# A hybrid attention and mLSTM layer: first stage in written order, pieces of the weights ahead of x, gate row before the gate chain, decays in halves, loads tied behind matmuls

## The chip, the cores and the metric

The kernel runs on one core of a Trainium2 chip. A core has five engines that work side by side: TensorE (PE) for matmuls, VectorE (DVE), ScalarE (ACT), GpSimd (POOL) and SyncE (SP), which here only issues DMAs. Each engine works off its own instructions in the order in which they were emitted, so an instruction that waits holds everything behind it on the same engine; that holds for a DMA issue on SP, ACT or POOL too. The metric is the device time of one execution in microseconds (us), the median of several runs; less is better.

## The reference

One layer for a sequence of 2048 tokens of width 1024, in float32:

```
c_act = silu(c)
shift, scale, gate = split(c_act @ w_ada + b_ada, 3)
h = rmsnorm(x, norm_w) * (1 + scale) + shift
proj = h @ w_in + b_in
na_q, na_k, na_v, na_z, ml_q, ml_k, ml_v, ml_o, ml_z, i_f, f_f, i_b, f_b = split(proj)
na_out = neighbourhood_attention(na_q, na_k, na_v, rpb) * silu(na_z)      # 32 x 64 grid, 8 heads
mq, mk = split(silu(short_conv(concat(ml_q, ml_k), conv_w, conv_b)))
hm = mlstm(mq, mk, ml_v, i_f, f_f) + flip(mlstm(flip(mq), flip(mk), flip(ml_v), flip(i_b), flip(f_b)))
ml_out = layernorm(hm * sigmoid(ml_o)) * ml_norm_w * silu(ml_z)           # 4 heads of 128
out = rmsnorm(x + gate * (concat(na_out, ml_out) @ w_out), final_norm_w)
```

## The kernel before

Every large product is made of three matmuls in a reduced float32 type: each operand is split into a high part (a rounded copy) and a low part (the rest), and high x high, high x low and low x high are added up in PSUM. So h is kept as hhi and hlo in four groups of 512 tokens, and a weight block as whi and wlo in one of two slots (a and b). A block of w_in is 256 columns; `load_w` (line 188) brings it in two halves, each a DMA, a high copy on ACT and a subtraction on POOL.

**First stage** (`start`, line 198). Shift and scale come from w_ada in 32 pieces of 128 x 512 (`ada_tile`, line 232): DVE multiplies each by a column of silu(c) and adds it to `acc`; at the end of a quarter `columns` (line 242) sums `acc` over the partitions with four matmuls against ones, and ACT, POOL or DVE add the bias and, for the scale, 1 and norm_w, into shT and gT. There are four quarters: (part, q) with part 1 the scale, part 0 the shift, and q the half of the 1024 features. x comes in sixteen tiles of 128 tokens; `prep_x` (line 217) squares them on ACT, takes the reciprocal root by Newton steps (`rsqrt`, line 1181; on POOL for the first four tiles, on DVE else) and scales x. PE transposes the scaled x feature by feature, and h = gT * x + shT is written as hhi (ACT) and hlo (POOL or DVE). For group 0 the first four features' tiles are done (`first_h`, line 264) and multiplied into four PSUM tiles (`vo_first`, line 473) before the other half of shift and scale is there (`scaled`, `shifted`). For later groups `make_h` (line 282) runs as a side chain: while `vo_group` (line 485) makes the products of block 1 with group g, each of its four token tiles advances the chain by a step that makes two features of h of group g + 1. `vo_group` evacuates each PSUM tile on DVE (line 499) into a staging tile of two, which is stored to DRAM when it is next flushed.

**Token blocks** (`tok_blocks`, line 557): blocks 2 to 5, four groups of four token tiles each; each token tile advances `self.chain` by one step (64 in all). The chain was the gate chain (decay logarithms, scans, line 577) and then `decays` (line 685): 16 groups of 128 x 1024 with two tiles, each loaded by two broadcast DMAs on SP, masked on POOL, raised by eight ACT exponentials and stored by two DMAs on ACT's queue. Between its steps ran `gate_row` (line 391), the third part of shift, scale and gate: eight 128 x 1024 pieces of w_ada in two buffers, summed on DVE. In the same time SP issues the small copies that build the bias tables (lines 528 and 551).

**Convolution blocks** (`conv_blocks`, line 752): blocks 6 to 9, eight tiles of 24 matmuls over 512 tokens each, a five tap convolution on DVE, SiLU on ACT, and for k a transpose on PE (line 819).

**mLSTM stage** (`phase1b`, line 929): per head two passes over chunks of 128 tokens, with the remaining projections (`nq_gen`, line 845) pumped between them as filling for PE. `close_step` (line 990) runs once per chunk and finishes older chunks; it also takes a job at every other step: eight loads of finished keys (`kk_jobs`, line 974). The gate values z come back in one tile (`load_z`, line 1063), are multiplied into the result, and the tile is stored to d_mix on ACT's queue (line 1155).

**Attention and output** (`phase2`, line 1206) follow in an order written by hand.

What sets the order: outside `manual_schedule` a planner places the instructions of each engine, by its own costs and estimates of when inputs are ready; tile releases and DMA landings become waits. Inside `manual_schedule` each engine gets its instructions as they are written. Before, only the last stage (line 1591) was in written order. The first stage began so:

```python
        for tt in range(4):
            load_x(tt)
        prep_x([0, 1, 2, 3])
        for kt in range(KT):
            ada_tile(1, 0, kt)
            if kt == 2:
                nc.sync.dma_start(bada, self.b_ada)
                nc.sync.dma_start(nw, self.norm_w)
        self.load_w(0, 0, (0,))
```

## Time and profile before

| | us |
|---|---|
| median of 3 runs | 1383.26 (1382.79 to 1388.96) |
| the profiled execution | 1385.16 |
| its span, first to last instruction | 1383.4 |
| PE busy in it | 1291.3 |
| mean granted clock of PE | 0.989 of full speed |

In the rows below PE, DVE, ACT, POOL and SP are the engines, PEld is PE's loading of weights, and SPq or ACTq with a DMA name is the issue of a DMA on that engine. A row of a timeline gives the start, the duration, the engine, the line, the operation, out<-in with shapes, how many such instructions follow each other, and in brackets how long the engine had been idle and what released it. A row of waits gives who waited for whom, the sum, how often, and the longest. The granted clock is a share of TensorE's full clock.

### The profile page before, as it was taken

What the parts mean: (1) busy time and instruction counts of PE and PEld (TensorE: products, weight loads), DVE (VectorE), ACT (ScalarE), POOL (GpSimd) and SP (SyncE); (2) the same over time, 40 slices, a digit from 0 to 9 for tenths busy, and PEclk for the clock granted to TensorE, in tenths of its full rate; (3) what the DMA queues carried; (4) which work ended last, traced back from release to release, by engine and by line L of the source; (5) the groups of instructions that cost most, each with busy time, mean ns of one, the idle gap of its engine ahead of it and who ended that gap; (6) DMA issues with size and microseconds to landing.
All of it is one profiled execution on the core that took longest, in us unless ns stands there. A gap on an engine that the chain in (4) does not pass through costs nothing.

```text
span 1383.4 us, 23357 instructions
## 1 busy us (share of the span) xinstructions
PE 1291.3 (93%) x8204; PEld 1104.9 (80%) x8204; DVE 792.3 (57%) x2428; ACT 531.8 (38%) x1123; POOL 284.1 (21%) x306
## 2 busy tenths in 40 slices
PE   2989998998999999999989999899998999999996
PEld 2889998998887778788878878778876777778775
DVE  6683324111355569246767866767736666667664
ACT  4642334423232233213313322323346555555552
POOL 4343212424101011001212101212201211112121
PEclk9999999999999999999999999999999999999998
DMA  9799449787557685554675788555588996867871
GB/s 321 223 290 228 122 97 238 175 204 189 149 110 210 151 191 160 164 157 144 184 219 182 229 237 284 165 159 159 176 249 251 209 228 171 187 184 183 205 182 47
DMA packets 243272, 263.29 MB, mean 190 GB/s; under 512 B 31814, under 2 KB 200006, under 8 KB 243154
## 3 DMA queue, kind: packets, MB, share of 16 engines
q1 hardware_dynamic: 151774, 186.18, 49.8%
q0 software_dynamic: 20496, 36.21, 10.8%
q10 hardware_dynamic: 70884, 39.40, 9.9%
q8 instruction: 65, 1.06, 0.3%
q14 instruction: 53, 0.43, 0.1%
HBM read 177.18 MB, written 92.72 MB: 195 GB/s over the span
## 4 chain that ended last, share of the span: by engine, by line
PE 46%; DMA 11%; issue 4%; DVE 4%; POOL 1%; ACT 1%; ACTq 0%; SPq 0%; DVEq 0%; POOLq 0%
PE pq L866 19%; PE y L1429 9%; DMA tab<-d_t 4%; PE pT L1369 3%; PE pO L1384 2%; PE pS L1341 2%; PE pi L1090 2%; DMA kv<-d_ck 2%; PE px L1088 2%; PE pc L429 2%; PE pc L430 2%; PE pc L431 2%; DMA d_mix<-zt 2%; PE dc L1036 1%; DMA d_qna<-qst 1%
## 5 line engine op out<-in xcount | busy, mean ns | idle before, releaser
L866 PE MATMUL pq<-hhi,whi_a 128*128 128x512 f32 x512 | 208.6, 407 | 1.2 <-ACT u L773 0.8
L866 PE MATMUL pq<-hlo,whi_a 128*128 128x512 f32 x512 | 208.9, 408 | 0.0
L866 PE MATMUL pq<-hhi,wlo_a 128*128 128x512 f32 x512 | 208.2, 407 | 0.0
L866 PEld LDWEIGHTS pq<-hhi,whi_a 128*128 128x128 f32 x512 | 97.3, 190 | 18.9 <-ACT u L773 1.2
L866 PEld LDWEIGHTS pq<-hlo,whi_a 128*128 128x128 f32 x512 | 97.2, 190 | 16.8 <-issue 0.5
L866 PEld LDWEIGHTS pq<-hhi,wlo_a 128*128 128x128 f32 x512 | 97.3, 190 | 16.6
L1371 ACT ACTIVATE pt<-pT 96x384 f32<-96x384 f32 (+3 forms) x128 | 65.8, 514 | 84.5 <-PE pT L1369 81.3
L1350 ACT ACTIVATE pbuf<-pbuf,mn 128x480 f32<-128x480 f32 (+5 forms) x128 | 76.1, 595 | 54.1 <-DVE mn L1349 53.8
L1429 PE MATMUL y<-hhi,whi_a 128*128 128x512 f32 x256 | 90.6, 415 | 0.5 <-ACT whi_a L1399 0.5
L1429 PE MATMUL y<-hhi,wlo_a 128*128 128x512 f32 (+1 forms) x272 | 90.6, 399 | 0.2 <-ACT y L1436 0.2
L1349 DVE CUSTOM_DVE_ANT_0 pbuf<-pS,tab 128x480 f32<-128x480 f32 (+5 forms) x128 | 63.3, 540 | 40.3 <-PE pS L1341 29.6
L840 POOL TENSOR_TENSOR wlo_a<-rawq,whi_a 128x1024 fp32r<-128x1024 f32 x20 | 48.6, 2430 | 169.8 <-ACT whi_a L839 144.9
L1112 POOL TENSOR_TENSOR hm<-hm,ck 128x128 f32<-128x128 f32 x64 | 26.4, 413 | 260.3 <-DVE hm L1111 183.4
L429 PE MATMUL pvo<-whi_b,hhi 128*128 128x256 f32 x256 | 74.1, 289 | 5.7 <-DVE stvo L499 5.7
L1093 ACT ACTIVATE num<-px,gtile 128x129 f32<-128x129 f32 x120 | 38.3, 366 | 105.7 <-PE px L1088 88.0
L1020 DVE TENSOR_SCALAR wv<-kv,gtile 128x129 f32<-128x129 f32 x120 | 38.4, 329 | 67.1 <-DMA kv<-d_ck 33.5
L1369 PE MATMUL pT<-ident,pbuf 128*128 128x128 f32 (+2 forms) x416 | 66.8, 273 | 10.0 <-DVE pbuf L1361 8.5
L1369 PEld LDWEIGHTS pT<-ident,pbuf 128*128 128x128 f32 (+2 forms) x416 | 50.3, 136 | 31.9 <-issue 11.6
L430 PE MATMUL pvo<-wlo_b,hhi 128*128 128x256 f32 x256 | 72.8, 285 | 0.0
L431 PE MATMUL pvo<-whi_b,hlo 128*128 128x256 f32 x256 | 72.8, 284 | 0.0
L714 ACT ACTIVATE dec<-dec,gtile 128x128 f32<-128x128 f32 x128 | 42.0, 392 | 71.4 <-POOL dec L710 68.3
L499 DVE TENSOR_TENSOR stvo<-pvo,brow 128x256 f32<-128x256 f32 x64 | 26.5, 419 | 68.6 <-PE pvo L431 56.4
(295 smaller groups left out, 3432.6 us busy)
## 6 DMA issues: line engine op xcount, KB each, us to landing
ck<-d_ck SPq DMA_DIRECT2D x64, 384.5 KB
kv<-d_ck SPq DMA_DIRECT2D x120, 128.5 KB
rawq<-in_w_main_dram SPq DMA_DIRECT2D x28, 512.0 KB
raw<-in_w_main_dram SPq DMA_DIRECT2D x20, 512.0 KB
d_ck<-stvo SPq DMA_DIRECT2D x16, 514.0 KB
x<-in_x_dram SPq DMA_DIRECT2D x16, 512.0 KB
wada<-in_w_ada_dram SPq DMA_DIRECT2D x32, 256.0 KB
dec<-d_mneg SPq DMA_DIRECT2D x32, 256.0 KB
```

Of the source, the lines that this page charges most:

```text
L429: nc.tensor.matmul(ps, lhi(k), rhi(k), start=(k == 0), stop=False)
L430: nc.tensor.matmul(ps, lhi(k), rlo(k), start=False, stop=False)
L431: nc.tensor.matmul(ps, llo(k), rhi(k), start=False, stop=(k == KT - 1))
L714: nc.scalar.activation(t[:, d, o, :], t[:, d, o, :], AF.Exp, bias=self.cols["g"][:, d, h, c : c + 1])
L840: nc.gpsimd.tensor_tensor(lo[:, :, cs], raw, hi[:, :, cs].bitcast(F32), ALU.subtract)
L866: nc.tensor.matmul(patch_ps(ps) if patch else ps, w, self.htok(h, g, k, patch), start=(k == 0 and n == 0), stop=(k == KT - 1 and n == 2))
L1020: nc.vector.tensor_scalar(wv, tiles[d, i][:, 128:257], self.cols["w"][:, d, h, c : c + 1], None, ALU.mult)
L1349: nc.vector.tensor_tensor_reduce(pt[:, :nk], ps, tabs[place[u]][j][:, :nk], 1.0, 3e38, ALU.add, ALU.min, mn)
L1350: nc.scalar.activation(pt[:, :nk], pt[:, :nk], AF.Exp, bias=mn, scale=-1.0, accum_out=sums[:, j : j + 1])
L1369: nc.tensor.transpose(ps[:cs, i, :], U[u][j][:, i * cs : (i + 1) * cs], self.ident)
L1371: nc.scalar.activation(t[:cs, :nch, :], ps[:cs, :nch, :], AF.Copy)
L1429: nc.tensor.matmul(y, m[:, k, :], w[k][:, cs], start=(k == 4 and n == 0), stop=(k == 3 and n == 2))
```

## The change

The first stage runs in written order. The bias of shift and scale becomes row 0 of `acc`, which starts from zero, so that `columns` is one instruction; the w_ada pieces of the first quarter come ahead of x. `load_w` is parted into a load and later splits (`raw_w`). x of groups 1 and 2 (tokens 512 to 1535) lies in the tiles that later hold hhi of groups 2 and 3, so it can be loaded early. The squares of a group are taken at the start of the group before it, the roots and scaling under `vo_first`; `vo_first` now runs for group 3 too. In the token blocks the gate row comes first, then the gate chain, then decays in 32 halves with six tiles. `behind` adds an order edge without a semaphore: the planner may not place the load ahead of the last matmul emitted before it. Key loads get such an edge and come at every fourth step; zt is loaded on SP's queue.

```diff
     def phase1(self):
-        self.hhi = [ht012.tile([P, KT, GT], F32R, name=f"hhi{g}") for g in range(3)]
-        self.hlo = [ht012.tile([P, KT, GT], F32R, name=f"hlo{g}") for g in range(3)]
+        self.hpools = {g: ht012 for g in range(3)}
+        self.hhi, self.hlo = [], []
+        for g in range(2):
+            self.token_tiles(g)
...
-        self.start(left)
+        with self.tc.manual_schedule():
+            self.start(left)
...
+    def raw_w(self, blk, slot, halves=(0, 1)):
...
+        def part(half):
+            raw = self.raw.tile([P, 4, 256], F32, tag=f"raw{half}", name=f"raw_{blk}_{half}")
             nc.sync.dma_start(raw, self.w_main[blk, :, 4 * half : 4 * half + 4, :])
             ks = slice(4 * half, 4 * half + 4)
+            def run(eng=nc.gpsimd):
+                nc.scalar.activation(hi[:, ks, :256], raw, AF.Copy)
+                eng.tensor_tensor(lo[:, ks, :256], raw, hi[:, ks, :256].bitcast(F32), ALU.subtract)
+            return run
...
         def load_x(tt):
-            pool = early if tt // 4 == 2 else xp
-            t = pool.tile([P, D], F32, tag="x", bufs=4, name=f"x_{tt}")
+            g, j = divmod(tt, 4)
+            if g in (1, 2):
+                if j == 0:
+                    xs[g] = self.hpools[g + 1].tile([P, 4, D], F32, tag=f"hhi{g + 1}", name=f"xs_{g}")
+                t = xs[g][:, j, :]
+            else:
+                t = xp.tile([P, D], F32, tag="x", bufs=4, name=f"x_{tt}")
...
+        def columns(part, q, ps):
+            qs = slice(4 * q, 4 * q + 4)
+            if part:
+                nc.vector.scalar_tensor_tensor(self.gT[:, qs], ps, 1.0, nw[:, qs], ALU.add, ALU.mult)
             else:
+                nc.scalar.activation(self.shT[:, qs], ps, AF.Copy)
...
-        for tt in range(4):
-            load_x(tt)
-        prep_x([0, 1, 2, 3])
+        nc.vector.memset(acc, 0.0)
+        nc.sync.dma_start(cact, self.cT)
+        nc.scalar.activation(cact, cact, AF.Silu)
+        nc.scalar.dma_start(acc[0:1, :], self.b_ada)
+        nc.scalar.dma_start(nw, self.norm_w)
         for kt in range(KT):
             ada_tile(1, 0, kt)
+        for tt in four:
+            load_x(tt)
+        part = self.raw_w(0, 0, (0,))[0]
...
+        columns(1, 0, sums(1, 0))
+        rst = roots(four, squares(four))
+        part()
...
         for kt in range(KT):
             ada_tile(0, 1, kt)
+            if kt == 2:
+                columns(1, 1, ps)
+        parts = self.raw_w(1, 1)
...
+        for tt in range(4, 8):
+            load_x(tt)
+        for k in range(4, KT):
+            scaled(k)
+            if k == 4:
+                turned(7)
+        columns(0, 1, sums(0, 1))
         for k in range(4, KT):
             shifted(k)
             next(first)
+        parts[0]()
+        parts[1](nc.vector)
         ada_s.close()
+        self.hpools[3] = self.pool(left, "ht3", bufs=1)
+        for tt in range(8, 12):
+            load_x(tt)
         self.small_loads()
+        for tt in range(12, 16):
+            load_x(tt)
...
         for g in range(NG):
+            tiles = [4 * g + 4 + j for j in range(4)] if g < NG - 1 else []
+            if g in (1, 2):
+                self.token_tiles(g + 1)
+            ssq = squares(tiles) if tiles else None
+            self.chain = iter(())
+            if g:
+                for k, _ in enumerate(self.vo_first(g)):
+                    if k == 2:
+                        self.flush()
+                        next(fills, None)
+                    if k == 3 and tiles:
+                        rst = roots(tiles, ssq)
+                        for tt in tiles:
+                            scale_x(tt, rst)
+            self.vo_group(0, 0, g, True)
+            if g == 0:
+                rst = roots(tiles, ssq)
+                for tt in tiles:
+                    scale_x(tt, rst)
+            self.chain = next_h(tiles) if tiles else next_w()
...
             self.vo_group(1, 1, g)
...
     def gate_row(self, pool):
-        acc = pool.tile([P, D], F32, name="gsum")
+        acc = [self.dec_tile(pool, f"gsum_{j}") for j in range(2)]
...
+        for kt in range(3):
+            load(kt)
+        yield
...
+            if kt + 3 < KT:
+                load(kt + 3)
...
+    def dec_tile(self, pool, name):
+        return pool.tile([P, GT], F32, tag="decs", bufs=6, name=name)
...
     def tok_blocks(self, chain_pool):
-        self.chain = itertools.chain(self.gate_chain(chain_pool, self.gates), self.decays(chain_pool, self.gate_row(chain_pool)))
+        self.chain = itertools.chain(self.gate_row(chain_pool), self.gate_chain(chain_pool, self.gates), self.decays(chain_pool))
+        next(self.chain)
...
-            self.load_w(blk + 1, (blk + 1) % 2)
+            parts = self.raw_w(blk + 1, (blk + 1) % 2)
...
+                if g < 2:
+                    parts[g]()
...
     def decays(self, pool):
+            self.behind(nc.sync.dma_start(t, src.broadcast_to([P, 512])), self.mark)
...
+        for n in range(len(groups) + 3):
+            for step, fn in ((3, raised), (2, masked), (0, load)):
+                if 0 <= n - step < len(groups):
+                    fn(n - step)
             yield
...
     def conv_blocks(self, pool):
-                self.load_w(order[i + 1][0], (blk + 1) % 2)
+                parts = self.raw_w(order[i + 1][0], (blk + 1) % 2)
...
+                    if 2 <= 4 * sub + g < 2 + len(parts):
+                        parts[4 * sub + g - 2]()
...
+    def behind(self, step, other):
+        order = mybir.DependencyInfo(mybir.DependencyClass.NoSync, mybir.DependencyReason.DATA)
+        self.tc.add_manual_dep(step.ins, other.ins.name, order, reason="order alone")
...
     def kk_jobs(self):
-            self.nc.sync.dma_start(self.kk[ct][:, e * T + T // 2 : (e + 1) * T].bitcast(F32), src)
+            self.behind(self.nc.sync.dma_start(self.kk[ct][:, e * T + T // 2 : (e + 1) * T].bitcast(F32), src), self.mark)
...
     def close_step(self):
-        self.job(self.steps % 2)
+        self.job(self.steps % 4 == 0)
...
         def load_z(gi):
-            nc.scalar.dma_start(t, self.d_zml[4 * gi : 4 * gi + 4, :, h].rearrange("a p q -> p a q"))
+            nc.sync.dma_start(t, self.d_zml[4 * gi : 4 * gi + 4, :, h].rearrange("a p q -> p a q"))
```

More of the change, by code (lines that the diff above doesn't have):

```diff
@@ L181, in phase1, with token_tiles @@
         self.phase1b(left, right)
+    def token_tiles(self, g):
+        for part, held in (("hi", self.hhi), ("lo", self.hlo)):
+            held.append(self.hpools[g].tile([P, KT, GT], F32R, tag=f"h{part}{g}", name=f"h{part}{g}"))
     def stage_tile(self, name):
@@ L236, in ada_tile, with sums @@
             a = acc[:, c0 : c0 + GT]
-            if kt == 0:
-                nc.vector.tensor_scalar(a, w, cact[:, kt : kt + 1], None, ALU.mult)
-            else:
-                nc.vector.scalar_tensor_tensor(a, w, cact[:, kt : kt + 1], a, ALU.mult, ALU.add)
-        def columns(part, q):
+            nc.vector.scalar_tensor_tensor(a, w, cact[:, kt : kt + 1], a, ALU.mult, ALU.add)
+        def sums(part, q):
             ps = self.sp.tile([P, 4], F32, tag="sp", name=f"mod_{part}_{q}")
@@ L322, in start @@
                 turned(3)
+        part()
         for k in range(4):
@@ L326, in start @@
             if k == 2:
-                columns(1, 1)
+                ps = sums(1, 1)
             next(first)
@@ L417, in gate_row @@
             ps = self.sp.tile([P, GT], F32, tag="sp", name=f"gp_{j}")
-            nc.tensor.matmul(ps[0:1, :], self.ones[:, 0:1], acc[:, j * GT : (j + 1) * GT], start=True, stop=True)
+            nc.tensor.matmul(ps[0:1, :], self.ones[:, 0:1], acc[j], start=True, stop=True)
             yield
@@ new lines, in raised @@
+        def raised(n):
+            h, gi, d = groups[n]
+            t = tiles.pop(n).rearrange("p (c t) -> p c t", c=4)
+            for o in range(4):
+                c = 4 * gi + o
+                nc.scalar.activation(t[:, o, :], t[:, o, :], AF.Exp, bias=self.cols["g"][:, d, h, c : c + 1])
+            dst = self.d_ck[h, 4 * gi : 4 * gi + 4, :, 641 + d * CH : 641 + (d + 1) * CH].rearrange("c p t -> p c t")
+            nc.scalar.dma_start(dst, t)
+        for n in range(len(groups) + 3):
+            for step, fn in ((3, raised), (2, masked), (0, load)):
+                if 0 <= n - step < len(groups):
+                    fn(n - step)
+            yield
```

174 lines of the change are left out of this document (64 added, 110 removed).

## The prediction

> **What bounds the kernel now.** I read the page first, then the windows by stage, then what TensorE waited for, and only then the timelines around its gaps.
>
> ```profile
> span 1383.4 us, 23357 instructions
> PE 1291.3 (93%) x8204; PEld 1104.9 (80%) x8204; DVE 792.3 (57%) x2428; ACT 531.8 (38%) x1123; POOL 284.1 (21%) x306
> ```
>
> TensorE (PE) is the bound: 1291.3 of 1383.4 us. No edit removes a large matmul, so the change can win only what PE idles (1383.4 - 1291.3 = 92.1 us) and what it loses at a reduced clock. The windows say where both lie. The columns are the stretch, its length, the busy time of PE, PEld, DVE, ACT and POOL, the granted clock, the DMA share and GB/s.
>
> ```profile
> core 0: us, PE busy (x) PEld busy (x) DVE busy (x) ACT busy (x) POOL busy (x), PEclk, DMA share, GB/s
> 0.00:46.30 46.30, 20.21 (x113) 18.36 (x113) 28.87 (x38) 21.52 (x34) 22.32 (x35) 1.00 0.78 269
> 46.30:160.00 113.70, 105.76 (x857) 103.38 (x858) 62.02 (x137) 49.08 (x70) 46.93 (x41) 1.00 0.91 231
> 160.00:220.00 60.00, 60.00 (x505) 59.33 (x504) 22.80 (x62) 25.21 (x39) 10.45 (x10) 1.00 0.58 147
> 220.00:260.00 40.00, 34.30 (x272) 33.68 (x271) 11.15 (x15) 15.59 (x31) 7.38 (x6) 0.96 0.82 206
> 260.00:360.00 100.00, 93.50 (x751) 90.64 (x750) 13.70 (x35) 37.95 (x97) 37.27 (x16) 0.98 0.76 191
> 420.00:500.00 80.00, 73.78 (x323) 58.97 (x322) 42.98 (x77) 23.93 (x36) 10.90 (x4) 0.96 0.69 177
> 680.00:760.00 80.00, 76.06 (x417) 64.73 (x416) 54.20 (x216) 23.11 (x49) 16.51 (x16) 0.98 0.67 201
> 850.00:910.00 60.00, 50.78 (x269) 42.37 (x268) 43.18 (x171) 17.17 (x39) 11.26 (x13) 0.94 0.72 231
> ```
>
> Idle plus clock loss (length times one minus the clock) by stage: 26.1 until the second half of group 0 starts; 7.9 in the rest of the first stage; nothing in 160 to 220; 5.7 + 1.6 = 7.3 in 220 to 260; 6.5 + 2.0 = 8.5 in 260 to 360 (both in the token blocks); 6.2 + 3.2 = 9.4 in the convolution blocks; 3.9 + 1.6 = 5.5 and 9.2 + 3.6 = 12.8 in the mLSTM stage. From 1010 on nothing is edited. What ended the larger of PE's waits in the edited stages after the first:
>
> ```profile
> PE pv L429 <- DVE stv L464: 6.5, 3, 4.7
> PE kt L819 <- ACT acc_k L809: 6.2, 3, 4.3
> PE pvo L429 <- DVE stvo L499: 5.7, 3, 2.4
> ```
>
> Each names an engine that reads or feeds PSUM and is itself held by something else; the parts below follow it to that.
>
> **Part 1, the first stage in written order, until 46.3.**
>
> ```profile
> 18.01 4.27 ACT L228 ACTIVATE x<-x,rst 128x1024 f32<-128x1024 f32 x4 [7.28 <-POOL rst L1203]
> 18.81 5.48 DVE L240 SCALAR_TENSOR_TENSOR acc<-wada,cact,acc 128x512 f32<-128x512 f32 x7 [0.27 <-DMA wada<-in_w_ada_dram]
> 24.99 1.86 PE L246 MATMUL mod<-ones,acc 128*128 128x1 f32 x8 [0.26 <-ACT gT L249]
> 30.90 0.78 ACT L269 ACTIVATE hhi<-tp,shT,gT 128x512 fp32r<-128x512 f32 x1 [3.83 <-POOL shT L250]
> 31.73 0.59 PE L482 MATMUL pvo<-whi_a,hhi 128*128 128x272 f32 x1 [4.87 <-ACT hhi L269]
> 46.30 0.39 PE L482 MATMUL pvo<-whi_a,hhi 128*128 128x272 f32 x1 [1.21 <-ACT hhi L279]
> ```
>
> Before, the shift sums are ready at 24.99 + 1.86 = 26.85, yet ACT makes the first h at 30.90, because POOL works off low parts of the weights before it adds the bias to shT. Now the bias is a row of the accumulator and shT one ACT copy. x comes behind eight pieces of w_ada and is scaled later, but DVE takes the reciprocal root from POOL (ACT waited 7.28 us for it there). I reckon the scaling ends near 24, as it does now (18.01 + 4.27 = 22.3) or up to 2 us later, and the sums at 27.5, so h starts near 27.8, 3 us earlier. The memset of acc and its 8 KB row lie under the wait for w_ada.
>
> Not all of this survives. DVE's gT for the second half (columns(1, 1)) now stands after the third of the last eight accumulations, and waits for PE's sums, which stand behind two k-steps of matmuls. With PE 3 us earlier these come near 38.3. Queued behind on DVE are five accumulations, 5 x 5.48/7 = 3.9, so the sum is complete near 42.2. Four matmuls (4 x 1.86/8 = 0.9) and two ACT steps give a start of the second half near 44.3 instead of 46.30. **Gain 2.0** (bounds: -1 if x is 3 us late, +4 if DVE never waits for PE).
>
> **Part 2, the rest of the first stage.**
>
> ```profile
> 45.51 2.57 ACT L279 ACTIVATE hhi<-hg,shT 128x512 fp32r<-128x512 f32 x4
> 59.13 1.06 ACT L223 ACTIVATE junk<-x 128x1024 bf16<-128x1024 f32 x1
> 60.31 1.06 ACT L223 ACTIVATE junk<-x 128x1024 bf16<-128x1024 f32 x1
> 60.31 0.17 DVE L224 TENSOR_SCALAR ssq<-ssq 128x4 f32<-128x4 f32 x1 [1.27 <-ACT junk L223]
> 63.10 2.74 DVE L230 TENSOR_SCALAR x<-x,rst 128x1024 f32<-128x1024 f32 x4
> 345.55 0.58 PE L429 MATMUL pv<-whi_b,hhi 128*128 128x256 f32 x1 [4.66 <-DVE stv L464]
> 348.49 0.37 PE L430 MATMUL pv<-wlo_b,hhi 128*128 128x256 f32 x1
> ```
>
> Groups 2 and 3 profit: their x is loaded a group ahead, squared at the start of the group before, and scaled under the long vo_first; roots no longer sit between the h of make_h. Group 1 does not. In written order ACT does four shifted h (2.57, from 43.5), two weight pieces (about 1.06 each, like any 128x1024 copy) and then the squares (60.31 - 59.13 = 1.18 each): ready at 43.5 + 2.57 + 2.1 + 4.7 = 52.9. Roots on DVE take 63.10 - 60.31 = 2.8, scaling 2.74: 58.4. PE has 48 matmuls of 272 columns and 24 of 256 until then, at 60/505 = 0.119 us per 256: 44.3 + 6.1 + 2.9 = 53.3. It waits about 4.8 (the first transposes go ahead). A gap of this length is followed by half speed, as after 345.55, until 348.49: 3 us, of which half is lost. So 6.3 in place of 7.9: **gain 1.6** (bounds: -5 if groups 2 and 3 stall as now, +7.9 if PE never waits).
>
> **Part 3, gate row first, decays in halves (220 to 360).**
>
> ```profile
> SPq L702 <- DMA d_ck<-dec: 66.4, 19, 8.7
> DVE gsum L410 <- DMA wide<-in_w_ada_dram: 23.8, 5, 10.3
> DVE stv L464 <- DMA d_vna<-stv: 52.4, 6, 14.9
> ```
>
> Two mechanisms. DVE stands up to 10.3 us at a gsum step whose piece of 128 x 1024 has not landed, with the evacuation behind it. And SP stands up to 8.7 us at a decay load whose tile (one of two) still waits for its store, with the d_vna store behind it, whose staging tile DVE then lacks. The change gives the gate row three kt ahead and runs it in block 2; it gives decays six tiles of half the size, each reused three steps after its store, and ties their loads behind the last matmul. The work is the same: 32 loads, 32 stores and 128 exponentials; the masks come in 32 halves instead of 16, and the gsum steps in 16 of 512 (0.78 each by the row of part 1) instead of 8 of 1024, on a DVE that is 13.70 of 100 us busy there and hides them. Steps: 13 + 16 + 35 = 64 of the 64 calls, so nothing runs over by more than a step or two; if it did, PE would wait about 3 us per step. Of 7.3 + 8.5 = 15.8 I take 11.5, as table DMAs stay on SP among the stores (bounds: -4, +15.8).
>
> **Part 4, weight splits two groups later (420 to 500).**
>
> ```profile
> 475.47 20.97 SPq L551 DMA_DIRECT2D d_t<-d_e  x24
> 482.49 1.06 ACT L195 ACTIVATE whi_b<-raw 128x1024 fp32r<-128x1024 f32 x1 [5.93 <-DMA raw<-in_w_main_dram]
> ```
>
> ACT stands 5.93 us at a split whose raw piece is on its way among 24 table DMAs; behind it is the Silu of acc_k, and PE waits for that. Now the split is written two tiles of 24 matmuls (512 columns, 24 x 2 x 0.119 = 5.7 us each) later, 11 us after its load. ACT's wait should go; the table DMAs and stores remain. Of 9.4 I take 6.0 (bounds: -2, +9.4).
>
> **Part 5, zt on SP, keys at every fourth step.**
>
> ```profile
> 859.75 0.47 SPq L981 DMA_DIRECT2D hhi<-d_kna  x1
> 854.43 0.37 ACTq L1155 DMA_DIRECT2D d_mix<-zt  x1
> 866.34 0.37 ACTq L1070 DMA_DIRECT2D zt<-d_zml  x1
> 866.81 0.69 ACT L900 ACTIVATE qst<-pq,bcol 128x512 fp32r<-128x512 f32 x1 [10.72 <-DMA hhi<-d_kna]
> SPq L1058 <- POOL hm L1112: 131.5, 57, 3.8
> ```
>
> zt has one tile. Its load stands on ACT's queue behind the store of its last content, issued at 854.43; among key loads of 128 x 1024 floats (one of them at 859.75) that takes until 866.34, and ACT's evacuations stand 10.72 us. The load moves to SP, and the key loads are spread to half the rate. That is the larger part of the 12.8 lost in 850 to 910. The 5.5 in 680 to 760 have other causes. SP pays: it waits 57 times already for a free ck tile, and now also for the d_mix store. I take **+6.0** net (bounds: SP below, +12.8).
>
> The Trainium skill speaks against this move: "DMA: Bandwidth & Descriptors", section "Queues, rings and completion order", says that each DMA engine serves its queues in turn, so a load on ACT's queue overtakes what SP has queued and one on SP's does not. By that page alone I would halve part 5 to 3 and say 1360 (an estimate of mine); no row of before shows a zt load on SP.
>
> **Sum.** 2.0 + 1.6 + 11.5 + 6.0 + 6.0 = 27.1. The profiled execution took 1385.16 (span 1383.4 and 1.8 around it), 1.9 above the median of 1383.26; 1385.16 - 27.1 = 1358.1, at the median 1356.2. I say **1357**; with each part's doubt its own range is 1346 to 1367.
>
> **Rivals.**
>
> *Waits only move* (0.20). The planner still sets the order from block 2 on, with its own costs. If the stores stay late behind the table DMAs, parts 3 and 4 bring half (9) and part 5 nothing: 1385 - 12 = 1373. For it: 52.4 us of DVE's wait is for a store that SP issues among tables. Against: the holds of 66.4 us on SP are named by the trace.
>
> *Nearly all goes* (0.13). PE never waits for group 1, and parts 3 to 5 reach their upper bounds: 2 + 7.9 + 15.8 + 9.4 + 12.8 = 48, 1337. Against: x of group 1 depends on ACT as shown.
>
> *Nothing gained* (0.08). Group 1 and the later groups cost what parts 4 and 5 bring: 1376 to 1390. Half a per cent, 6.9 us, is about what a measurement of this kernel tells from no change.
>
> *SP becomes the bound of the mLSTM stage* (0.14, slower). Each zt load (one for each of four heads' four groups, but the last) now holds SP for as long as the d_mix store takes, with ck, kv and the matrices queued behind. This is the place of the skill's rule above; the price is from rows.
>
> ```profile
> 640.40 1.63 PE pq L866 x7
> 644.54 1.63 PE pq L866 x7
> 814.35 5.65 DMA kv<-d_ck
> ```
>
> A chunk takes 644.54 - 640.40 = 4.1 us; ck is fetched three chunks ahead, 12.4, less about 5.65 to land: 6.8 us of cover. It decides from the point where a hold passes that. At 866.34 - 854.43 = 11.9 the excess is 5.1 plus 2 at half speed, 7 us; if six of the loads do this, 42: 1357 + 42 = 1399. For it: the 11.9. Against: it was measured among key loads that are now spread.
>
> The likeliest has 0.45. Faster by over 0.5%: 0.45 + 0.20 + 0.13 = 0.78; same 0.08; slower 0.14. The range 1338 to 1387 leaves out the slower case and the low edge of the best one.
>
> **What would show it.** Part 1: the second half of group 0 near 44, and DVE waiting for PE's sums near 34 to 38. Part 2: one PE gap of 4 to 6 us near 53, its releaser the scaled x, and none of over 1 us in the later groups. Part 3: SP's wait for d_ck<-dec far under 66.4, and PE's waits for stvo and stv under 3 together. Part 4: no wait of 4.3 for acc_k. Part 5: no ACT hold over 10 us in 840 to 910, but more wait on SP. It is wrong if the gaps turn up in PE's waits under new names (DVE wv <- DMA kv, SP at zt), or if the written first stage ends later than now.

## The result, and the profile after

| | before | after |
|---|---|---|
| median of 6 runs each, us | 1383.03 (1381.01 to 1388.96) | 1372.41 (1370.58 to 1375.86) |
| ratio | | 0.9922, 95% interval 0.9900 to 0.9945 |
| span of the profiled execution, us | 1383.4 | 1371.5 |
| PE busy in it, us | 1291.3 | 1293.8 |

The kernel became 10.6 us faster, inside the range, but the forecast was 1357: 27.1 were to be won. The first lines of after's page:

```profile
span 1371.5 us, 23403 instructions
PE 1293.8 (94%) x8204; PEld 1108.7 (81%) x8204; DVE 795.9 (58%) x2451; ACT 518.1 (38%) x1112; POOL 275.0 (20%) x302
```

Its windows by stage, with the columns of the prediction; the first two are parted where the second half of group 0 starts:

```profile
0.00:49.98 49.98, 19.85 (x112) 18.06 (x113) 36.33 (x52) 21.68 (x33) 12.56 (x13) 0.96 0.82 279
49.98:160.00 110.02, 102.79 (x780) 100.92 (x781) 56.78 (x139) 42.81 (x64) 34.27 (x37) 0.93 0.85 225
160.00:220.00 60.00, 59.35 (x484) 56.73 (x483) 25.21 (x50) 15.20 (x17) 15.16 (x11) 1.00 0.46 133
220.00:260.00 40.00, 40.00 (x337) 39.74 (x336) 9.27 (x36) 7.38 (x11) 0.32 (x3) 1.00 0.40 111
260.00:360.00 100.00, 100.00 (x813) 98.48 (x812) 13.54 (x33) 45.41 (x127) 48.96 (x35) 1.00 0.92 224
420.00:500.00 80.00, 75.09 (x328) 60.07 (x327) 45.82 (x80) 23.94 (x36) 11.68 (x4) 0.96 0.73 187
840.00:910.00 70.00, 65.57 (x361) 55.20 (x360) 57.83 (x215) 21.49 (x48) 15.45 (x16) 1.00 0.75 223
```

The token blocks are what the forecast wanted: PE is busy for all of 220 to 360, at full clock. The first stage is worse (clock 0.93 behind 49.98, where it was 1.00), and 420 to 500 still loses 4.9 us and some clock. Both kernels run the same large matmuls in the same order, so the start of the n-th one in the two traces shows where time went (after minus before; on the right the same for two executions from the experiments, `c_before_again` and `b_after_again`):

```
stage (large matmuls)           forecast   first pair   second pair
first stage        (to  768)      -3.6        +9.1         +7.0
token blocks       (to 2304)     -11.5       -15.6        -14.9
convolution        (to 3072)      -6.0        +5.0         -0.5
mLSTM              (to 4500)      -6.0        -8.8         -8.5
rest of the span                    0         -1.6         +4.9
sum                              -27.1       -11.9        -12.0
```

Two stages failed, the first and the convolution blocks; of the latter the 5.0 in the first pair is not repeated in the second. What TensorE waited for in after:

```profile
PE mod L270 <- DVE acc L264: 15.4, 2, 12.8
PE tp L285 <- ACT x L255: 10.9, 4, 9.3
PE dc L1096 <- DVE wv L1080: 8.8, 7, 2.3
PE kt L875 <- ACT acc_k L865: 6.1, 5, 2.1
...
PE tp L310 <- DVE h L314: 3.2, 1, 3.2
```

Of the waits for stvo and stv 0.7 is left, kt's waits for acc_k are as long as before (6.2 in 3, now 6.1 in 5). The first line leads to the first stage. DVE's timeline there:

```profile
6.52 6.26 DVE L264 SCALAR_TENSOR_TENSOR acc<-wada,cact,acc 128x512 f32<-128x512 f32 x8 [3.37 <-DMA acc<-in_b_ada_dram]
14.75 0.16 DVE L276 SCALAR_TENSOR_TENSOR gT<-mod,nw 128x4 f32<-128x4 f32 x1 [1.96 <-PE mod L270]
17.63 0.17 DVE L248 TENSOR_SCALAR ssq<-ssq 128x4 f32<-128x4 f32 x1 [2.72 <-ACT junk L243]
...
19.63 2.19 DVE L1260 TENSOR_TENSOR nwt_x<-rst 128x4 f32<-128x4 f32 x1
21.86 0.38 DVE L1261 TENSOR_TENSOR nwt_x<-nwt_x,ssq 128x4 f32<-128x4 f32 x1
...
22.55 20.50 DVE L264 SCALAR_TENSOR_TENSOR acc<-wada,cact,acc 128x512 f32<-128x512 f32 x19
42.96 0.16 DVE L276 SCALAR_TENSOR_TENSOR gT<-mod,nw 128x4 f32<-128x4 f32 x1
43.08 3.90 DVE L264 SCALAR_TENSOR_TENSOR acc<-wada,cact,acc 128x512 f32<-128x512 f32 x5
```

The first and the last row of the last 24 accumulations in before:

```profile
18.05 0.49 DVE L238 TENSOR_SCALAR acc<-wada,cact 128x512 f32<-128x512 f32 x1 [1.54 <-DMA wada<-in_w_ada_dram]
...
34.01 8.16 DVE L240 SCALAR_TENSOR_TENSOR acc<-wada,cact,acc 128x512 f32<-128x512 f32 x7
```

In after DVE stands behind the first eight: for PE's sums (1.96), then for the squares of x (2.72), which are late because x is loaded behind eight pieces of w_ada; then come the roots. The other 24 accumulations start at 22.55 and end at 46.98. Before, they ran from 18.05 to 42.17: 24.1 us there and 24.4 here, so they are simply 4.5 late. PE has its sums for gT at 38.3 + 0.95, but DVE gets to gT only at 42.96 and does not wait for it. What this does to PE, in its timeline, and then the windows from 40 to 60:

```profile
38.30 0.95 PE L270 MATMUL mod<-ones,acc 128*128 128x1 f32 x8
...
43.89 0.66 PE L285 MATMUL tp<-ident,x 128*128 128x128 f32 x4 [1.06 <-ACT hg L297]
47.13 1.83 PE L270 MATMUL mod<-ones,acc 128*128 128x1 f32 x8 [2.58 <-DVE acc L264]
49.98 0.59 PE L537 MATMUL pvo<-whi_a,hhi 128*128 128x272 f32 x1 [1.02 <-ACT hhi L302]
```

```profile
40.00:45.00 5.00, 3.49 (x27) 3.03 (x26) 4.89 (x6) 1.85 (x4) 1.71 (x1) 1.00 0.80 257
45.00:50.00 5.00, 1.85 (x9) 1.80 (x9) 1.95 (x4) 1.54 (x4) 0.00 (x0) 0.57 0.78 276
50.00:55.00 5.00, 5.00 (x20) 4.72 (x21) 4.01 (x5) 4.97 (x8) 2.21 (x1) 0.50 0.75 292
55.00:60.00 5.00, 5.00 (x38) 5.00 (x38) 3.23 (x11) 4.76 (x8) 0.28 (x3) 0.91 0.94 321
```

The second half of group 0 starts at 49.98 in place of 46.30, 3.7 us late, and runs at half clock until 56, which costs another 5 x (0.50 + 0.09) = 3.0 us: its 48 matmuls are done 6.2 us late (the next one starts at 58.95 in place of 52.72). In before the clock is 1.00 in all four windows; in `c_before_again` it is 0.78 and 0.88 in the second and third. In after it falls twice more in this stage, to 0.66 in 65 to 70 and to 0.53 and 0.79 in 100 to 110.

### The profile page after: what moved, and what is told of

Same layout as the page of the kernel before. It is cut to its first block, busy times and chain, and to the rows that moved or that the text cites. A ratio compares the mean times of both kernels' runs of the same rounds, so it can differ in the third digit from the quotient of the medians.

```text
span 1371.5 us, 23403 instructions
## 1 busy us (share of the span) xinstructions
PE 1293.8 (94%) x8204; PEld 1108.7 (81%) x8204; DVE 795.9 (58%) x2451; ACT 518.1 (38%) x1112; POOL 275.0 (20%) x302
## 3 DMA queue, kind: packets, MB, share of 16 engines
q8 instruction: 65, 1.06, 0.3%
## 4 chain that ended last, share of the span: by engine, by line
PE 48%; DMA 8%; DVE 5%; issue 3%; ACT 1%; POOL 1%; ACTq 0%; SPq 0%; POOLq 0%; DVEq 0%
PE pq L922 20%; PE y L1489 10%; DMA tab<-d_t 3%; PE pT L1429 3%; PE pO L1444 2%; DMA kv<-d_ck 2%; PE pS L1401 2%; PE pi L1150 2%; PE px L1148 2%; PE pc L484 2%; PE pc L486 2%; PE pc L485 2%; PE dc L1096 1%; DMA d_qna<-qst 1%; PE a L1135 1%
## 5 line engine op out<-in xcount | busy, mean ns | idle before, releaser
L896 POOL TENSOR_TENSOR wlo_a<-rawq,whi_a 128x1024 fp32r<-128x1024 f32 x20 | 48.6, 2428 | 153.8 <-ACT whi_a L895 115.7
L1153 ACT ACTIVATE num<-px,gtile 128x129 f32<-128x129 f32 x120 | 38.3, 364 | 108.5 <-PE px L1148 90.1
L769 ACT ACTIVATE dec<-dec,gtile 128x128 f32<-128x128 f32 x128 | 42.2, 393 | 54.8 <-POOL dec L762 48.2
```

Source lines behind the costliest of these rows:

```text
L769: nc.scalar.activation(t[:, o, :], t[:, o, :], AF.Exp, bias=self.cols["g"][:, d, h, c : c + 1])
L896: nc.gpsimd.tensor_tensor(lo[:, :, cs], raw, hi[:, :, cs].bitcast(F32), ALU.subtract)
L1153: nc.scalar.activation(num[:, d, :], px[:, d, :], AF.Copy, scale=self.cols["inter"][:, d, h, c : c + 1])
```

## The experiments

Each group of runs (a to e) had the kernel before beside it, whose median was 1374 to 1376, so kernels are compared by their ratio to it. The interval of a ratio is some 0.003 either way, that of a difference of two some 0.004, or 5 to 6 us; most differences below are near that.

| run | median us | ratio | 95% interval |
|---|---|---|---|
| b_after_again | 1364.31 | 0.9923 | 0.9898 to 0.9949 |
| c_before_again | 1374.42 | 0.9990 | 0.9961 to 1.0019 |
| a_first_as_before | 1358.25 | 0.9875 | 0.9841 to 0.9910 |
| a_decays_as_before | 1372.25 | 0.9974 | 0.9947 to 1.0001 |
| a_split_as_before | 1364.18 | 0.9915 | 0.9875 to 0.9954 |
| a_zt_keys_as_before | 1370.54 | 0.9964 | 0.9937 to 0.9991 |
| b_roots_later | 1366.45 | 0.9941 | 0.9916 to 0.9967 |
| b_x_first | 1360.99 | 0.9897 | 0.9868 to 0.9926 |
| b_split_after_scaling | 1362.75 | 0.9919 | 0.9889 to 0.9949 |
| c_x_first_roots_on_gpsimd | 1361.86 | 0.9907 | 0.9871 to 0.9943 |
| c_no_fills_in_group_0 | 1366.96 | 0.9941 | 0.9919 to 0.9964 |
| c_zt_on_act | 1360.78 | 0.9900 | 0.9869 to 0.9931 |
| d_splits_held_back | 1359.06 | 0.9884 | 0.9862 to 0.9906 |
| d_keys_as_before | 1364.99 | 0.9934 | 0.9912 to 0.9957 |
| d_first_as_before_zt_on_act | 1359.35 | 0.9880 | 0.9857 to 0.9903 |
| d_and_splits_held_back | 1355.73 | 0.9859 | 0.9833 to 0.9885 |
| e_part_3_alone | 1367.27 | 0.9936 | 0.9908 to 0.9963 |
| e_written_stage_mended | 1359.50 | 0.9877 | 0.9849 to 0.9905 |

**One part undone at a time.** Each is the kernel after with one part of the change taken back. First stage (`start` and what it calls from before):

> The first stage as in the kernel before; gate row, decays, weight splits, zt and keys as in the kernel after. By the count of matmuls in the two traces the written first stage costs some 9 us and hides what the rest gains: then this kernel ends near 1363. By the prediction (parts 1 and 2 gain 3.6) it would be slower than the kernel after, near 1376. If the gains of block 2 on only make good what the first stage left in disorder, 1370 to 1374.

0.0048 under the kernel after, 6.6 us: the written first stage is a loss, and the rest of the change alone would have been worth 17 us (0.0125 x 1375). Gate row, gate chain and decays:

> The kernel after with gate row, gate chain and decays in the old order and size, and the weights of the token blocks split at once. By the count of matmuls part 3 brings 15.7: 1388. By the prediction 11.5: 1384. If the later end of the decays is what the convolution blocks pay for (rival), about 5 come back there and the gain is 10.7: 1383, with the first evacuation of the convolution near 364 on the clock of before.

0.0051 or 7.0 us lost, less than all three figures, though by the count of matmuls the token blocks alone take 12.0 us longer than in `b_after_again`. The rival's place does not show it: the convolution blocks take nearly the same time with either order of the decays (here 0.5 longer than in `c_before_again`, in `b_after_again` 0.5 shorter). Weight splits:

```diff
-                parts = self.raw_w(order[i + 1][0], (blk + 1) % 2)
+                self.load_w(order[i + 1][0], (blk + 1) % 2)
...
-                    if 2 <= 4 * sub + g < 2 + len(parts):
-                        parts[4 * sub + g - 2]()
```

> The kernel after with the weight splits of the convolution blocks written at the top of the block, as before. By the prediction part 4 brings 6: 1378. By the count of matmuls the convolution blocks lose 5 in place of gaining: if the later split is the reason, 1367; if it is the decays, whose stores end at 365 in place of 349, or if the planner puts the splits where they were anyhow, the time is that of the kernel after, 1371 to 1374.

No difference that the intervals show: the later splits bring nothing that can be measured. Last, zt and keys:

```diff
-            nc.sync.dma_start(t, self.d_zml[4 * gi : 4 * gi + 4, :, h].rearrange("a p q -> p a q"))
+            nc.scalar.dma_start(t, self.d_zml[4 * gi : 4 * gi + 4, :, h].rearrange("a p q -> p a q"))
-        self.job(self.steps % 4 == 0)
+        self.job(self.steps % 2)
```

> The kernel after with zt loaded on ACT's queue, keys at every second step and without their order edges. By the prediction 6 and by the count of matmuls 7 to 9 slower than the kernel after: 1378 to 1381, with an ACT hold of some 10 us behind zt or the keys in 840 to 910. If that hold was an accident of the order before, 1371 to 1374.

0.0041 or 5.7 us lost, as forecast, and the hold is back (10.48 us, shown below).

**Controls.** The two kernels themselves:

> The kernel after, unchanged, beside the next three on one chip, so that they are compared with it and not with the kernel before alone: ratio to the kernel before 0.99 to 0.995. Where its convolution blocks again lose some 5 us against the kernel before, that loss belongs to the change; where they gain, it was that one execution.

> The kernel before, unchanged, for a trace of it on the chip that ran the others. If the convolution blocks of the kernel after gain some 4 to 6 us against it here (as five executions suggest, against the trace first shown), part 4's stage was disturbed in that one execution of the kernel after; if they lose, the loss of 5 is the change's.

The ratio of after holds, 0.9923. In these traces its convolution blocks neither gain 4 to 6 nor lose 5, but gain 0.5, so the loss of 5 in the first trace does not repeat. Single executions differ by as much: in the twelve runs of this section that leave these blocks as in after they take 188.7 to 197.0 us.

**The first stage.** Roots behind the second eight accumulations:

```diff
-        rst = roots(four, squares(four))
+        ssq = squares(four)
+        for kt in range(KT):
+            ada_tile(0, 0, kt)
+        rst = roots(four, ssq)
...
-        for kt in range(KT):
-            ada_tile(0, 0, kt)
```

> The reciprocal roots of x written behind the second eight accumulations of w_ada on DVE. If DVE stands at the roots for the squares of x and the last accumulation sets the second half of group 0, the accumulations run on from 12.8, the second half starts at 44 to 46 in place of 50, and the kernel is 3 to 6 us under the kernel after. If the pieces of w_ada come too late for that (rival: the loads bind), DVE waits for wada instead, the second half stays near 50 and the time is the kernel after's.

The rival came, and more: DVE waited 3.8 for the next pieces of w_ada, x was scaled 7 us later, DVE then stood 8.1 for the sums of a later PE, and the second half started at 53.4. x first:

```diff
-        for kt in range(KT):
-            ada_tile(1, 0, kt)
         for tt in four:
             load_x(tt)
+        rst = roots(four, squares(four))
+        for tt in four:
+            scale_x(tt, rst)
+        for kt in range(KT):
+            ada_tile(1, 0, kt)
```

> x of group 0 loaded ahead of w_ada, and its roots written ahead of all accumulations. If waiting for x in the middle of DVE's order is the cause, the roots end near 14, 24 accumulations of 1.0 follow without a break, the second half starts at 41 to 44 and the kernel is 5 to 8 us under the kernel after. If the loads bind, the second half comes at 47 to 50, and the time changes by under 2.

The roots ended at 12.9, as the theory wanted, and yet the second half started at 49.6: DVE had the roots (2.7) ahead of its accumulations and a wait for PE's sums (1.96) in their midst. Not standing at x was not enough: the kernel was 3.6 us under the kernel after, within the interval. GpSimd's split moved:

```diff
+        for tt in four:
+            scale_x(tt, rst)
         part()
...
-        for tt in four:
-            scale_x(tt, rst)
```

> GpSimd's first low part of the weights (128 x 1024) written behind the scaling of x. If it held DVE's roots (one of 128 x 4 took 2.19 beside it), the roots take 2.8 in place of 5 and all behind them comes 2 us earlier: 2 us under the kernel after. If the hold only moves to an accumulation, nothing changes (under 1).

The roots took 2.8 in place of 5, but the 19 accumulations behind them took 22.6 in place of 20.5 and the second half started at 49.8: the hold only moved. Next, x first, with the Newton steps on GpSimd and DVE's first gT three accumulations later:

```diff
-            self.rsqrt(xp, rst, ssq, f"x{tts[0]}")
+            self.rsqrt(xp, rst, ssq, f"x{tts[0]}", nc.gpsimd if tts[0] == 0 else None)
...
             ada_tile(0, 0, kt)
+            if kt == 2:
+                columns(1, 0, ps)
```

> x of group 0 ahead of w_ada, the Newton steps of its roots on GpSimd, and DVE's first gT behind three accumulations of the next quarter; all else as in the kernel after. If what DVE has to do ahead of its 32 accumulations (roots, waits for PE and x) sets the second half of group 0, the last accumulation ends near 42, the second half starts at 44 to 46, and the kernel is 4 to 6 us under the kernel after (ratio to the kernel before near 0.988). If the port that DVE shares with GpSimd takes all of it back, the second half stays at 49 to 50, as with x first alone.

The second half started at 48.4, between the two forecasts. PE now ran into the sums of the third quarter, written in the middle of its first matmuls, waited 2.5 there and lost the clock. That wait was taken away in the last run:

```diff
-            if k == 2:
-                ps = sums(1, 1)
             next(first)
+        ps = sums(1, 1)
...
-            if kt == 2:
+            if kt == 5:
                 columns(1, 1, ps)
```

> The kernel after with x ahead of w_ada, the Newton steps on GpSimd, PE's sums of the third quarter behind its first 48 matmuls, and the splits held back. If PE's wait inside its written order at 36 and the half clock after it are what was left of the loss, that wait goes, the second half starts at 46 to 48 at full clock, and the ratio is 0.983 to 0.986, level with the planner's first stage. If DVE's work alone sets it, the wait moves to the second half (48 to 50) and the ratio is 0.987 to 0.989.

This run's windows from 35 to 50, and then PE's timeline before the second half of group 0:

```profile
35.00:40.00 5.00, 5.00 (x43) 5.00 (x42) 4.95 (x3) 0.05 (x1) 4.44 (x2) 1.00 0.77 240
40.00:45.00 5.00, 1.90 (x16) 1.61 (x15) 4.55 (x7) 1.76 (x4) 0.00 (x0) 0.98 0.72 231
45.00:50.00 5.00, 3.98 (x16) 3.61 (x17) 2.31 (x4) 3.90 (x8) 0.00 (x0) 0.50 0.98 385
```

```profile
43.98 0.66 PE L286 MATMUL tp<-ident,x 128*128 128x128 f32 x4 [2.88 <-ACT hg L298]
47.71 0.59 PE L539 MATMUL pvo<-whi_a,hhi 128*128 128x272 f32 x1 [1.02 <-ACT hhi L303]
```

PE now does its first 48 matmuls by 40.2 without a wait between them, and stands behind them instead; the second half starts at 47.71, but at half clock, and 0.9877 fits the second theory. Since this run holds the splits back too, it is compared with d_splits_held_back (0.9884): the mended stage brings 1 us, within the interval (by the count of matmuls the first stage is 2.5 us shorter). In the three orders with x first DVE stands only 0.7 to 2.0 us between its first accumulation and its last, which ends at 44.7 to 46.6 us.

**The fills.** In after one more gap stands at 98. SP's queue there, and GpSimd's memset of the staging tile that DVE needs next:

```profile
82.91 3.95 SPq L593 DMA_DIRECT2D d_t<-big  x2
86.95 4.68 SPq L561 DMA_DIRECT2D d_ck<-stvo  x1
...
100.34 0.10 POOL L543 MEMSET stvo<- 128x4 f32 x1 [17.42 <-DMA d_ck<-stvo]
```

```diff
-            for _ in range(2 if g < NG - 1 else 0):
+            for _ in range(2 if 0 < g < NG - 1 else 0):
```

> The kernel after without the two table fills at the end of group 0; they come at the end of the first stage instead. If the store of group 0 stands behind them and its tile is what DVE waits for near 98, the PE gap there (1.7 to 3.2) goes and the kernel is 2 to 4 us under the kernel after; if the fills then hold the first loads of the token blocks, the gap near 148 grows from 1.4 by as much and the time stays.

The gap at 98 went and the gap near 148 grew from 1.4 to 3.8, so the second case: at either place the fills cost a gap.

**The splits, held in place.** The order edge of the change, used on ACT, one group later:

```diff
-                    nc.scalar.activation(u[:, 2 : GT + 2], ps, AF.Identity, bias=bias)
+                    evac = nc.scalar.activation(u[:, 2 : GT + 2], ps, AF.Identity, bias=bias)
...
-                    if 2 <= 4 * sub + g < 2 + len(parts):
-                        parts[4 * sub + g - 2]()
+                    if 3 <= 4 * sub + g < 3 + len(parts):
+                        self.behind(parts[4 * sub + g - 3](), evac)
```

> The kernel after with order edges that put each weight split of the convolution blocks behind ACT's evacuation of the fourth and fifth group, so that the planner can't write it ahead of its raw piece. If part 4 failed because the planner moved the splits forward again, ACT's waits for raw (3 to 5 in the third block) go, PE's waits for acc_k fall from 4 to 6 us to under 2, the convolution blocks gain 3 to 6 us against the kernel after, and the ratio to the kernel before comes to 0.988 to 0.990. If PE's waits there are set by DVE's own work and not by the splits, the ratio stays near 0.992.

0.9884, 5.4 us under the kernel after. ACT's timeline where the fourth block's weights are split, in after and then in this run:

```profile
478.25 0.68 ACT L827 ACTIVATE u<-pc,bcol 128x512 f32<-128x512 f32 x1
482.65 1.06 ACT L211 ACTIVATE whi_b<-raw 128x1024 fp32r<-128x1024 f32 x1 [3.72 <-DMA raw<-in_w_main_dram]
483.61 0.58 ACT L877 ACTIVATE stk<-kt 128x512 f32<-128x512 f32 x1
484.09 1.05 ACT L211 ACTIVATE whi_b<-raw 128x1024 fp32r<-128x1024 f32 x1
485.04 0.71 ACT L865 ACTIVATE acc_k<-acc_k,cb 128x512 f32<-128x512 f32 x1
```

```profile
470.73 0.72 ACT L866 ACTIVATE acc_k<-acc_k,cb 128x512 f32<-128x512 f32 x1 [1.78 <-DVE acc_k L865]
471.36 0.67 ACT L828 ACTIVATE u<-pc,bcol 128x512 f32<-128x512 f32 x1
471.93 1.05 ACT L211 ACTIVATE whi_b<-raw 128x1024 fp32r<-128x1024 f32 x1
```

In after both splits stand ahead of a Silu of acc_k, and the first waits 3.72 for its piece. In the code they are written behind the Silu of the last acc_k, the second a group later than the first; the planner put both ahead of it, with one evacuation between them. Held back, they wait for nothing, and PE's waits for acc_k fall to 2.0 in 3. The edge and the later group were not tried apart.

**zt's queue and the pace of the keys.** One of the two taken back at a time (the lines of the diff above):

> The kernel after with zt alone back on ACT's queue; keys stay at every fourth step. If part 5's gain of about 6 is zt's change of queue, 1368 to 1371 on the clock of this chip (ratio to before near 0.996) and the PE gap of 5 near 850 is back. If it is the keys' slower pace, the time of the kernel after (near 0.992) with no such gap.

> The kernel after with keys at every second step and without their order edges; zt stays on SP. If the pace of the keys alone brings part 5, the kernel is 5 to 6 us slower than the kernel after (ratio near 0.996), as with both undone, and PE's gap of 5 near 850 is back or turns into a wait on SP. If zt on SP does as well without it, the ratio stays at 0.990 to 0.993.

Neither lost measurably against after (0.9900 and 0.9934 beside 0.9923), only both together do (0.9964); 0.9934 is not told from 0.9964 either. ACT's timeline with both taken back, and with zt alone on ACT's queue:

```profile
837.06 0.37 ACTq L1215 DMA_DIRECT2D d_mix<-zt  x1
...
848.67 0.37 ACTq L1130 DMA_DIRECT2D zt<-d_zml  x1
849.14 0.69 ACT L956 ACTIVATE qst<-pq,bcol 128x512 fp32r<-128x512 f32 x1 [10.48 <-DMA d_mix<-zt]
```

```profile
841.38 0.37 ACTq L1215 DMA_DIRECT2D d_mix<-zt  x1
...
844.03 0.37 ACTq L1130 DMA_DIRECT2D zt<-d_zml  x1
```

With keys at every second step SP issues six key loads between 831 and 843, and zt's tile is free 11.6 us after the store's issue; at every fourth it issues none between 815 and 849, and the tile is free after 2.65 us. So with slow keys the store lands early, and with zt on SP nobody on ACT stands behind it. But then SP does. Its waits in the mLSTM stage of `d_keys_as_before`, and PE in the same run:

```profile
SPq L1130 <- DMA d_mix<-zt: 43.4, 14, 6.4
```

```profile
853.23 0.80 PE L1135 MATMUL a<-ck 128*128 128x128 f32 x2 [2.26 <-DMA ck<-d_ck]
```

SP loads zt at 847.01, and the ck that it issues behind, after one more key load, comes late: PE waits 2.26 for it (with both edits taken back its gap there is 5.2), and the clock is 0.83 in 850 to 860. That is the wait on SP that the expectation named. With zt alone on ACT's queue PE has no wait near 850.

**Do the parts add up?**

> The first stage as before, zt on ACT's queue, all else as after. The first stage as before gave 0.9875 and zt alone on ACT 0.990 where the kernel after gives 0.992: if the two add up, 0.985 (1355 beside 1375); if zt's queue makes no difference, 0.9875.

> The run before this one with the weight splits held back as well. If all three add up, 0.981 to 0.984 (1349 to 1353 beside 1375); if the splits bring nothing, the time of the run before this one.

> The kernel before with part 3 alone: gate row first, decays in halves with order edges, weights of the token blocks split a group later. By the prediction 11.5 faster than the kernel before, a ratio of 0.9917; by the count of matmuls 12 to 15 (0.989 to 0.991). If undoing it (a ratio of 0.9974 in place of 0.9923, 7 us) is the right measure, 0.995.

zt's queue makes no difference (0.9880 beside 0.9875). With the splits held back the kernel comes to 0.9859, the best of all: 19 us under the kernel before and 9 under the kernel after. That is 2.9 for the splits, between the two forecasts. Part 3 alone brings 0.0064 x 1375 = 8.8. The count of matmuls shows where each run won or lost (us in each stage, one execution each):

| run | first stage | token blocks | convolution | mLSTM |
|---|---|---|---|---|
| c_before_again | 153.8 | 202.5 | 192.2 | 462.0 |
| b_after_again | 160.8 | 187.6 | 191.7 | 453.4 |
| a_first_as_before | 153.3 | 190.4 | 188.7 | 455.4 |
| a_decays_as_before | 159.0 | 199.5 | 192.7 | 454.6 |
| a_zt_keys_as_before | 159.8 | 187.1 | 191.4 | 461.2 |
| c_zt_on_act | 158.2 | 186.8 | 197.0 | 455.4 |
| d_keys_as_before | 159.5 | 187.1 | 191.8 | 456.7 |
| d_splits_held_back | 160.4 | 187.2 | 190.5 | 454.4 |
| d_and_splits_held_back | 153.2 | 190.2 | 188.1 | 456.5 |
| e_part_3_alone | 151.9 | 190.8 | 192.3 | 460.7 |
| e_written_stage_mended | 157.9 | 187.2 | 188.8 | 452.4 |

The written first stage costs some 7 us in its own stage, of which 3 come back in the token blocks. Part 3 is worth 11.7 to 12.0 in the token blocks. With the splits held back the convolution blocks take 189.1 in the mean of three, in the twelve runs as in after 192.5.

## Why the prediction failed

**Part 1 failed, and is the larger error.** Its first step was "the sums at 27.5, so h starts near 27.8". The second eight accumulations, behind DVE's wait for x and the roots, end only near 28.8; the sums end at 28.96 + 1.82 = 30.78, and h starts at 31.03, no earlier than before (30.90). The step that decided was: "Queued behind on DVE are five accumulations ... so the sum is complete near 42.2". It let DVE stand at gT waiting for PE's sums of 38.3. The sums came at 38.30, which is luck: h was 3.2 later than forecast, but PE ran at its full pace from 35 on, where in before it did so from 38. And DVE was not there: I had followed PE's order and x's way to ACT ("the scaling ends near 24 ... or up to 2 us later"; it ended at 26.9) and had costed the roots on DVE only for x, not for the 24 accumulations queued behind them. They start 4.5 late and the second half 3.7 late where 2.0 early was forecast; the half clock behind it adds 3.0. The experiments take the first theory a step further: moving x out of the way is not enough, because roots, waits for PE and GpSimd's holds stand in the same queue; before, the roots were on GpSimd, and DVE's last quarter ended at 42.2. That "the written first stage ends later than now" was named as a sign of being wrong.

**Part 2** forecast one gap of 4 to 6 near 53, and got 1.30 at 62 and three of 0.33 behind it, released by the scaled x as said. That it is short is luck: PE, due at 53.3, came 8.7 late itself, and x, due at 58.4, was scaled only near 65. "none of over 1 us in the later groups" was wrong (3.23 at 98, behind fills and a store on SP). "Groups 2 and 3 profit" does not show in the count: from the 96th large matmul to the end of the stage after takes 2.9 us longer than before (1.6 in the second pair), where 1.6 was to be won, and 1.5 and 2.1 lie in the matmuls of groups 2 and 3. The stage as a whole loses 6.6 where parts 1 and 2 were to win 3.6.

**Part 3 was right in its mechanism.** PE's waits in 160 to 355 fell from 12.2 to 0.7. 11.5 was forecast; the count gives 11.7 to 12.0 in the token blocks, the medians 8.8 alone and 7.0 by undoing it, which their intervals do not tell from 11.5. SP's wait for d_ck<-dec fell less than said, from 66.4 to 47.4; with six tiles it no longer reaches the evacuations.

**Part 4 failed because the change does not do what it says**, a rival that I had not set up. The step was "ACT's wait should go". The planner kept the splits ahead of what they were to follow. Held in place by an edge, a group later, they bring 5.4 in one pair of runs and 2.9 in another, and 3.3 by the count, where 6.0 was forecast. The mechanism was right; the size came out at half to nine tenths.

**Part 5 was right**: 5.7 for 6.0. No ACT hold over 10 us is left in 840 to 910; the longest is 6.6. The rival that SP becomes the bound needed holds of more than 6.8 at zt, and priced them at 11.9. SP's waits in the mLSTM stage of after show what came:

```profile
SPq L1118 <- POOL hm L1172: 132.1, 54, 4.1
...
SPq L1130 <- DMA d_mix<-zt: 35.7, 13, 4.7
```

The longest wait for the store is 4.7, since the keys are spread; with keys at the old pace it is 6.4, and PE's wait of 2.26 for ck shows that the rival's mechanism is real, at a lower price. The Trainium skill ("DMA: Bandwidth & Descriptors", section "Queues, rings and completion order") spoke against zt on SP, since each DMA engine serves the two queues in turn; the trace agrees with that page only in that the queues share the engines: a small store on ACT's queue took 11.6 us until its tile was free among SP's key loads.

The rival "Waits only move" gave 1373, the time that came, but not for its reason: it had parts 3 and 4 bring half and part 5 nothing, and no loss in the first stage. The sum of the measured parts is -6.6 + 7.0 to 8.8 + 0 + 5.7, or 6 to 8, for 10.6 measured; what is left is within the intervals. Not settled is why the mended first stage cannot reach the planner's. GpSimd's holds, below, are the likeliest: in before they lengthen the accumulations by some 5.4 us, in the mended run by 7.9, mainly because the second split of the weights (2.85) starts at 36.59 in their midst and in before at 43.98 behind them; the last accumulation ends 2.5 later (44.71 and 42.17). But no run took the holds away.

## What to carry to other kernels

When a stage is put into written order, follow each engine's own queue, not only the path of the data: an instruction that waits for a late input must not stand ahead of long work on an engine that is nearly full, as DVE is here, and moving it is not enough if other short work takes its place in the queue. Where a planner still sets the order, writing an instruction later does not make it later; look at the emitted order, or tie it with an edge. When two edits remove one hold, undo them singly before giving either the credit.

## What the runs showed of the hardware

DVE's accumulation takes 0.75 us alone, but up to 2.8 beside GpSimd. In after, a DVE operation on 128 x 4 (0.16 us alone) lasted until the end of the subtraction that GpSimd had begun just before it; both of their timelines:

```profile
19.45 2.35 POOL L212 TENSOR_TENSOR wlo_a<-raw,whi_a 128x1024 fp32r<-128x1024 f32 x1 [18.13 <-ACT whi_a L211]
...
19.63 2.19 DVE L1260 TENSOR_TENSOR nwt_x<-rst 128x4 f32<-128x4 f32 x1
```

Both end at 21.8. The Trainium skill ("SBUF — State Buffer", section "SBUF: two separate sides") says that a GpSimd operation that reads SBUF and a DVE operation with two inputs in SBUF contend for a shared pair of ports, and that the one that starts first holds it for the whole instruction; the trace agrees. 24 accumulations at 0.75 would be 18 us and took 24.4.

The clock fell to half without one long gap. In after it read 1.00, 0.83 and 0.50 in the microseconds from 44 to 47: it fell 1.1 us into a wait of 2.58, with a wait of 1.06 and four transposes ahead of that, and stayed at 0.50 until near 56. In the run with x first and the roots on GpSimd it fell (0.60 in 38 to 39) some 2 us into a wait of 2.51.

A window's 1.00 early in the trace does not show the pace. In before, PE's matmuls of 272 columns start 0.23 us apart until 38 and 0.13 apart from there on, and the windows on both sides read 1.00.
